# A second branch's output projection as two quads of seven products, with halves at both ends and a re-planned order

## The chip, the cores and the metric

The kernel runs on one core of a Trainium2 chip. The metric is the device time of one execution in microseconds (us); the time before is the median of three runs, 931.83 us (931.75 to 931.88).

## What is computed

One layer of a decoder trunk for 512 tokens of 1024 channels, in float32: three branches from one input projection, merged by gates, then a projection, then a feed-forward block, with RMS norms between.

```
h = rmsnorm(x);  proj = h @ w_in                    # 1024 -> 9216 columns
y_a = (gb * conv3(gc * v)) @ w_a_out                # branch 0
u   = conv31(u * sigmoid(ug)) + bias                # branch 1
y_b = silu(layernorm(u)) @ w_b_out
y_c = attention(q, rmsnorm(mem) @ w_kv) @ w_att_out # branch 2, 256 memory tokens
merged = sigmoid(p_g0)*y_a + sigmoid(p_g1)*y_b + sigmoid(p_g2)*y_c
x = x + merged @ w_o
x = x + (silu(gt) * up) @ w_down                    # gt, up: conv3 of rmsnorm(x) @ w_up, 2 x 2816
out = rmsnorm(x)
```

## The kernel before

**Numbers in two parts.** TensorE (PE) multiplies rounded operands (fp32r), so every operand is split: a high part, which is a rounding copy made by ScalarE (ACT), and a low part, the rest, made by a subtraction on VectorE (DVE). One product of two blocks is then three matmuls: high x high, high x low, low x high. For a weight unit of 128 x 1024 numbers this is `split_job` (L421): `high` (L444, ACT, tile `whi`) and `low` (L448, DVE, tile `wlo`). Where `lo_from` is given, ACT writes the negated high part instead, and a DMA issued by GpSimd's queue (POOL) adds the raw weights to it on the way, which leaves the low part.

**Seven products instead of eight.** The large projections run as quads: 1024 x 512 by 512 tokens is cut 2 x 2 x 2, and seven products of 24 matmuls of 256 columns (`multiply`, L612, matmul at L624) replace eight. The operands are sums of blocks: `form_jobs` (L527) makes them for the activations (t5, t7, t6, t4 are sums, b00, b10, b11 plain blocks), and `quad_loads` (L576) for the weights, either by DVE additions or, with `by_dma`, by accumulating DMAs from POOL's queue (`more`, L582). `quad_reads` (L643) puts the seven results from the PSUM banks together: copies on ACT (r1, r5, r6, r4), additions on DVE (r2, r7, r3).

**Order of the stages on PE.** Warm-up matmuls; keys and values of the memory (`keys_product`, `values_product`); eighteen mixer quads, with attention placed between their products; after the quads of the gates the output projections of the branches: `merge_product` (L1339) for branches 2 and 0, and, after the last product of the last gate quad, branch 1. A branch's projection is eight units, (m, g), of 24 matmuls of 512 columns each (L1349 to L1351). The conv over 31 taps runs on ACT and DVE beside the quads; its layer norm ends with two rows of statistics ("v") that PE brings to all partitions (L759), shortly before branch 1's projection: `lns` (L1261, DVE) scales, `swish` (L1268, ACT) applies the silu in place, `split_pair` (L1278 high, L1282 low) makes `ybh` and `ybl`. Behind each m come `weigh` (the gate times the bank, L1382) and `sum` into `mg` (L1400).

**From there on.** w_o as seven products a, b, f, c, d, e, g in this order (`pe_wo`, through `product`, L395 to L397; weights held in the freed operand tiles of the quads; `mgh` and `mgl` at L1500 and L1505; `ms` subtractions; rows x1 at L1560), the norm's transposes (L1586), eleven up quads whose start is written out by hand in `first`, conv3 and silu, then w_down as seven products with the rows read as they end (`read`, L1977), squared (L1982), a root (L1996), scaled on ACT and DVE (L2003, L2004) and written (L2008).

**What sets the order.** PE's order is a list written by hand (`seq`, and the table `beside`). All other work is a job with an engine, a cost, its inputs and its buffers; class `Jobs` (L99) places the jobs one after another on SP's queue, POOL's queue, ACT and DVE: `latest_starts` (L141) works back from PE's list when each is due, tables `LATER` and `AHEAD` shift kinds of jobs, `jobs.first` sets the first loads, and `transfer_end` models the two queues of transfers with the share `SHARE`. The instructions are issued in the order found, and each engine keeps it on the chip (`issue_in_program_order`, L81). So a wait of one instruction holds all that stand behind it on its engine.

## Time and profile before

| | |
|---|---|
| median of three runs | 931.83 us |
| the profiled execution | 931.52 us |
| its span, first to last instruction | 929.3 us |
| granted TensorE clock | 0.997 |
| PE busy | 916.8 us, 6644 matmuls |
| DVE busy | 837.3 us, 948 instructions |
| ACT busy | 672.5 us, 908 instructions |
| POOL busy | 126.5 us |
| DMA | 190.59 MB, mean 205 GB/s |

A row of the timeline has start, length, engine, line and operation, output and inputs, partitions x elements, a count where alike instructions are put together, and in brackets the idle time before it with what ended it. `bank` is a PSUM tile, `wf` a raw weight unit, `f..h` and `f..l` the parts of an operand. Lengths of matmuls overlap, since the next one starts before the last has drained; their starts tell the pace. The row of a stretch has its length, the busy time and count for each engine, the granted clock, the mean share of the 16 DMA engines and GB/s.

### The profile page before, as it was taken

The numbers are of one execution on the slowest core, as the hardware profiler recorded it, in microseconds if no ns is written. First come the engines' busy times: TensorE is split into PE (matmuls) and PEld (weight loads), VectorE is DVE, ScalarE is ACT, GpSimd is POOL, SyncE is SP. The second block draws the span as 40 slices with busy tenths as digits, with TensorE's granted clock in tenths as the row PEclk, the third lists the DMA queues.
The fourth block names the chain that finished last, engine by engine and source line by source line (L and its number), as shares of the span: only waits on it lengthen the run. The fifth ranks groups of instructions, "written<-read, shape, count | busy, mean of one in ns | idle before, by whom it ended". The sixth has DMA issues, their size and how long they took to land.

```text
span 929.3 us, 16689 instructions
## 1 busy us (share of the span) xinstructions
PE 916.8 (99%) x6644; PEld 860.5 (93%) x6644; DVE 837.3 (90%) x948; ACT 672.5 (72%) x908; POOL 126.5 (14%) x153
## 2 busy tenths in 40 slices
PE   8999999999999999999999999999999999999996
PEld 7999999999989999999899888898999999988885
DVE  6898999969889999999996778897899889999986
ACT  7676988759978879878856743766767676765655
POOL 0121111101111112110100011021211121002300
PEclk9999999999999999999999999999999999999998
DMA  9999678857676799967955598499999878779962
GB/s 356 371 269 236 137 171 178 201 133 136 170 185 170 177 191 243 210 174 183 226 115 158 186 314 179 97 246 295 258 226 235 209 141 166 195 268 329 251 125 91
DMA packets 54077, 190.59 MB, mean 205 GB/s; under 512 B 6128, under 2 KB 6256, under 8 KB 54000
## 3 DMA queue, kind: packets, MB, share of 16 engines
q0 software_dynamic: 20880, 75.24, 45.5%
q1 hardware_dynamic: 32400, 113.23, 34.0%
q8 instruction: 52, 0.85, 0.4%
q10 hardware_dynamic: 720, 1.06, 0.3%
q14 instruction: 25, 0.20, 0.1%
HBM read 185.31 MB, written 4.19 MB: 204 GB/s over the span
## 4 chain that ended last, share of the span: by engine, by line
PE 93%; DMA 3%; ACT 2%; DVE 1%; issue 1%; SPq 0%; ACTq 0%; POOLq 0%
PE bank L624 56%; PE bank L395 6%; PE bank L397 6%; PE bank L396 6%; PE bank L1349 5%; PE bank L1350 5%; PE bank L1351 5%; DMA wf<-in_w_up 2%; PE bank L871 2%; DMA mem<-in_mem_t 1%; ACT whi L444 0%; DVE wlo L448 0%; PE ss L750 0%; PE bank L1098 0%; ACT j L1982 0%
## 5 line engine op out<-in xcount | busy, mean ns | idle before, releaser
L444 ACT CAST whi<-wf 128x1024 fp32r<-128x1024 f32 (+1 forms) x195 | 202.9, 1044 | 100.9 <-PE bank L624 40.1
L448 DVE TENSOR_TENSOR wlo<-wf,whi 128x1024 fp32r<-128x1024 f32 (+1 forms) x189 | 228.3, 1214 | 29.8 <-ACT whi L444 29.4
L1170 ACT ACTIVATE tp<-u,pk 128x510 f32<-128x510 f32 (+22 forms) x184 | 119.7, 706 | 7.5 <-DVE acc L1177 6.5
L1177 DVE TENSOR_TENSOR acc<-acc,tp 128x1022 f32<-128x1022 f32 (+22 forms) x92 | 109.5, 1193 | 4.2 <-ACT tp L1170 2.4
L582 POOL DMA_DIRECT2D wf<-in_w_in x48 | 42.5, 894 | 229.7 <-DVE wlo L448 164.0
L624 PE MATMUL bank<-ft6h,wlo 128*128 128x256 f32 x232 | 64.4, 278 | 1.2 <-DVE wlo L448 1.2
L624 PE MATMUL bank<-ft6h,whi 128*128 128x256 f32 x232 | 64.6, 278 | 1.0 <-ACT gt L651 1.0
L624 PE MATMUL bank<-fb10h,whi 128*128 128x256 f32 x232 | 64.4, 278 | 0.0
L624 PE MATMUL bank<-fb00h,whi 128*128 128x256 f32 x232 | 64.4, 278 | 0.0
L624 PE MATMUL bank<-fb00l,whi 128*128 128x256 f32 x232 | 64.3, 277 | 0.0
L624 PE MATMUL bank<-fb00h,wlo 128*128 128x256 f32 x232 | 64.3, 277 | 0.0
L624 PE MATMUL bank<-ft7h,whi 128*128 128x256 f32 x232 | 64.3, 277 | 0.0
L624 PE MATMUL bank<-ft7l,whi 128*128 128x256 f32 x232 | 64.3, 277 | 0.0
L624 PE MATMUL bank<-ft7h,wlo 128*128 128x256 f32 x232 | 64.3, 277 | 0.0
L624 PE MATMUL bank<-fb11h,whi 128*128 128x256 f32 x232 | 64.3, 277 | 0.0
L624 PE MATMUL bank<-ft5h,wlo 128*128 128x256 f32 x232 | 64.2, 277 | 0.0
L624 PE MATMUL bank<-ft5h,whi 128*128 128x256 f32 x232 | 64.2, 277 | 0.0
L624 PE MATMUL bank<-ft5l,whi 128*128 128x256 f32 x232 | 64.2, 277 | 0.0
L624 PE MATMUL bank<-ft6l,whi 128*128 128x256 f32 x232 | 64.2, 277 | 0.0
L624 PE MATMUL bank<-fb10h,wlo 128*128 128x256 f32 x232 | 64.2, 277 | 0.0
L624 PE MATMUL bank<-fb10l,whi 128*128 128x256 f32 x232 | 64.2, 277 | 0.0
L624 PE MATMUL bank<-fb11l,whi 128*128 128x256 f32 x232 | 64.1, 276 | 0.0
(392 smaller groups left out, 3143.8 us busy)
## 6 DMA issues: line engine op xcount, KB each, us to landing
wf<-in_w_in SPq DMA_DIRECT2D x52, 512.0 KB, 4.9
wf<-in_w_in POOLq DMA_DIRECT2D x48, 512.0 KB, 5.8
wf<-in_w_up SPq DMA_DIRECT2D x29, 512.0 KB, 5.3
wf<-in_w_up POOLq DMA_DIRECT2D x28, 512.0 KB, 6.9
wf<-in_w_down SPq DMA_DIRECT2D x15, 512.0 KB, 4.2
wf<-in_w_v SPq DMA_DIRECT2D x8, 512.0 KB, 10.1
wf<-in_w_att_out SPq DMA_DIRECT2D x8, 512.0 KB, 3.9
wf<-in_w_a_out SPq DMA_DIRECT2D x8, 512.0 KB, 3.8
```

The costliest lines, as they stand in the source:

```text
L395: nc.tensor.matmul(ps, s_hi, w_hi, start=start, stop=False, skip_group_check=again)
L396: nc.tensor.matmul(ps, s_hi, w_lo, start=False, stop=False, skip_group_check=again)
L397: nc.tensor.matmul(ps, s_lo, w_hi, start=False, stop=stop, skip_group_check=again)
L444: nc.scalar.copy(parts[0], src())
L448: nc.vector.tensor_tensor(lo, src(), hi.bitcast(F32), op=ALU.subtract)
L582: nc.gpsimd.dma_start(out=tiles[key], in_=block(w, col[c], k), accum_op=ALU.add)
L624: nc.tensor.matmul(ps[:, c, :], w[:, k, at], a[k], start=first and n == 0, stop=i == 3 and n == 2, skip_group_check=again,)
L1170: nc.scalar.activation(two(("tp", p, s))[:, j, s:], two(("u", p))[:, j, : SEQ - s], AF.Copy, scale=weight(j),)
L1177: nc.vector.tensor_tensor(a, a, two(("tp", p, s))[:, :, s:], op=ALU.add)
L1349: nc.tensor.matmul(ps, w_hi[:, i, at], hi, start=first, stop=False)
L1350: nc.tensor.matmul(ps, w_hi[:, i, at], lo, start=False, stop=False)
L1351: nc.tensor.matmul(ps, w_lo[:, i, at], hi, start=False, stop=last)
```

## The change

1. Branch 1's projection leaves `merge_product`: its 1024 columns become two quads `("mq", 0)` and `("mq", 1)` through `quad_loads` (with `by_dma`), `multiply_job` on operand forms "y", and `quad_reads` without its last read. PE's order is f = 1, 5, 2, 6, 7, 4, 3, both quads in turn. The forms are made in halves of 512 columns (`y_parts`), the sums in place on `acc`.
2. `weigh` works on half the tokens of both channel blocks, from the tile `("y", m)`, once directly from the bank with a factor of -1.
3. Four low parts of w_o (products a and b) come by DMA (`WO_LOWS`).
4. The values' first unit (`V0`) is loaded, split and multiplied in halves, as the keys' first unit was before; `msq` waits for the high part of the values' second unit; `exp` waits for all four `sg`.
5. The last product "g" of w_down writes its second row tile into two banks of 256 columns, which are read, squared and summed by halves; row tile 1 is scaled after the read of row tile 0 of "g".
6. The planner: when a transfer is placed, the landing of the other queue's running transfer is set anew; ties are broken in a fixed order; some assumed costs differ (`SHARE`, `LOAD`, `MORE`, latencies), `LATER` and `AHEAD` have 91 entries instead of 24, `jobs.first` and the list `first` of the up quads are changed. The order on ACT, DVE and both queues is therefore different throughout.

```diff
-    for p in range(4):
-        split_pair(("acc", p), ("ybh", p), ("ybl", p), [("swish", p)])
+    def rows_of(p, r):
+        return two(("acc", p))[:, :, r * HALF : (r + 1) * HALF]
+    def y_parts(key, e, src, after, use):
...
+        def high():
+            if e == 0:
+                form_tile("y", key)
+            for at, h in pieces(form["y", key, "views"][0]):
+                nc.scalar.copy(h, src()[:, at, :])
+        def low():
+            hi, lo = form["y", key, "views"]
+            for (at, h), (_, l) in zip(pieces(hi), pieces(lo)):
+                nc.vector.tensor_tensor(l, src()[:, at, :], h.bitcast(F32), op=ALU.subtract)
...
+    for e in range(2):
+        top, end = ("acc", e), ("acc", 2 + e)
+        b00 = y_parts("b00", e, lambda e=e: rows_of(e, 0), done(e), [top])
+        b10 = y_parts("b10", e, lambda e=e: rows_of(2 + e, 0), done(2 + e), [end])
+        y_parts("b11", e, lambda e=e: rows_of(2 + e, 1), done(2 + e), [end])
...
+        job(Y5 + (e,), "DVE", dve(512), y5, ...)
+        job(("y", "t7", e), "DVE", dve(512), ...)
+        job(("y", "t6", e), "DVE", dve(512), ...)
+        job(("y", "t4", e), "DVE", dve(512), ...)
+        y_parts("t5", e, t5_half, [Y5 + (e,)], [Y5])
+        y_parts("t7", e, lambda e=e: rows_of(e, 1), [("y", "t7", e)], [top])
+        y_parts("t6", e, lambda e=e: rows_of(e, 0), [("y", "t6", e)], [top])
+        y_parts("t4", e, lambda e=e: rows_of(2 + e, 0), [("y", "t4", e)], [end])
...
+                quad = ("mq", m // 2)
+                if m % 2 == 0:
+                    quad_loads(quad, w_b_out, m * 256, m * 256 + 256, by_dma=True, lows=MQ_LOWS)
+                    quad_reads(quad, ("y", m), ("y", m + 1), ANY, all_but_4=True)
...
+                    def weigh_last(m=m, gate=gate, at=at, quad=quad):
+                        t = two(gate)[:, :, at]
+                        nc.vector.scalar_tensor_tensor(
+                            t, halves(("bank", quad, "a")), -1.0, t, op0=ALU.mult, op1=ALU.mult)
...
-        (GATE[1, 1], 3): lambda: [pe_merge(1, m) for m in range(4)],
+        (GATE[1, 1], 3): lambda: [
+            multiply_job(("mq", q), f, "y") for f in (1, 5, 2, 6, 7, 4, 3) for q in range(2)],
...
+    WO_LOWS = [(p, i) for p in "ab" for i in range(2)]
...
-            split_job(("wo", p, i), ("wo", key, i), 2, 512, [after], held=WO_HELD.get((p, i)))
+            split_job(("wo", p, i), ("wo", key, i), 2, 512, [after], held=WO_HELD.get((p, i)),
+                      lo_from=WO_SRC[p][i] if (p, i) in WO_LOWS else None)
...
+    halved_unit(K0, block(w_kv, 0, 0), 4)
+    halved_unit(V0, w_v[0, 0], 2)
...
+        if (hp, kp) == (0, 0):
+            for e in range(2):
+                pe(V0 if e else ("V0",), 6 * MM, lambda e=e: values_product(0, 0, e),
...
-        job(("msq", g), "ACT", actv(1024), mem_square, [("ldm", g, 0), ("ldm", g, 1)],
+        job(("msq", g), "ACT", actv(1024), mem_square,
+            [("ldm", g, 0), ("ldm", g, 1), ("wh", ("V", 0, 1))],
...
-                [("top", h, tp)] + ([("exp", h, 0)] if tp else []),
+                [("top", h, tp)] + ([("exp", h, 0)] if tp else [("sg", p) for p in range(4)]),
...
+    def end_steps(us, i):
+        for u in us:
+            hi, lo = w_units["pd", "g", u]
+            for k in range(PAIR_UNITS[u].start, PAIR_UNITS[u].stop):
+                ps = make(end_banks[i]) if k == 0 else tiles[end_banks[i]]
...
+            job(("sr", t, 0), "ACT", 0.4, lambda: square(last, 0, ENDS[0], ss_end),
+                [("rd", "end", 0)])
+            job("ends", "DVE", 0.1, first_end, [("sr", t, 0), ("hd", t)])
+            job(("sr", t, 1), "ACT", 0.4, lambda: square(last, 0, ENDS[1]), [("rd", "end", 1)])
...
+        job(("sc", t), "DVE", 0.95, lambda t=t: scaled(t),
+            [("rt", t)] + ([("rd", "g", 0)] if t == 1 else []))
...
-    def transfer_end(self, queue, start, cost):
+    def moved(self, queue, start):
...
+                slowed = "POOL" if e == "SP" else "SP"
+                if self.work[slowed] > 0.0 and self.moved(slowed, start) > free[slowed]:
+                    other = moving[slowed]
+                    free[slowed] = self.moved(slowed, start)
+                    ends[other] = free[slowed] + self.jobs[other][4]
```

More of the change, by code (lines that the diff above doesn't have):

```diff
@@ L218, in run @@
                 self.left[name][0] += 1
+        free = {e: 0.0 for e in ["PE"] + sorted({j[0] for j in self.jobs.values()} - {"PE"})}
         pe.reverse()
@@ L829, in hybrid_block_kernel, with halved_unit, high, low @@
-    first_parts = []
+    K0, V0 = ("K", 0, 0), ("V", 0, 0)
+    def halved_unit(unit, src, n_k):
+        s, raw, parts = unit[0], ("raw", unit), []
+        job(("raw tile", s), "NONE", 0.0, lambda: make(raw), take=[(raw, "wf")])
+        for e in range(2):
+            at = slice(512 * e, 512 * (e + 1))
+            job(("ld0", s, e), "SP", 0.7, lambda at=at: nc.sync.dma_start(
+                out=tiles[raw][:, at], in_=src[:, at]), [("raw tile", s)],
+                LOAD_LATENCY, use=[raw])
+            def high(e=e, at=at):
+                if e == 0:
+                    parts.extend(
+                        wts.tile([P, 1024], F32R, tag=s, name=name(s)) for s in ("whi", "wlo"))
+                    w_units[unit] = [t.rearrange("p (k n) -> p k n", k=n_k) for t in parts]
+                nc.scalar.copy(parts[0][:, at], tiles[raw][:, at])
+            def low(at=at):
+                hi, lo = parts
+                nc.vector.tensor_tensor(
+                    lo[:, at], tiles[raw][:, at], hi[:, at].bitcast(F32), op=ALU.subtract
+                )
+            job(("wh0", s, e), "ACT", actv(512), high,
+                [("ld0", s, e)] + ([("wh0", s, 0)] if e else []), use=[raw])
+            job(("wl0", s, e), "DVE", dve(512), low, [("wh0", s, e)], use=[raw])
@@ L1754, in hybrid_block_kernel @@
             pe_wo(p, i)
+    ENDS = [slice(0, 256), slice(256, 512)]
+    end_banks = [("bank", "end", i) for i in range(2)]
     def chain(p):
@@ L1764, in pe_down @@
         if u == 0 and before:
-            needs += [("rd", before, t) for t in range(2)]
+            needs += [("rd", before, t) for t in range(1 if p == "g" else 2)]
+        if p == "g":
+            banks = banks[:1] + (end_banks if u in (1, 2) else [])
         n, ts = (ps.stop - ps.start) * 6 * MM, range(2)
```

258 lines of the change are left out of this document (169 added, 89 removed), and 15 rows, old and new, of tables (AHEAD, LATER).

## The prediction

> **What bounds the kernel now.** I read the page's shares and its chain first, then the waits of PE, then stretches of time, and then single rows.
>
> ```profile
> span 929.3 us, 16689 instructions
> ...
> PE 916.8 (99%) x6644; PEld 860.5 (93%) x6644; DVE 837.3 (90%) x948; ACT 672.5 (72%) x908; POOL 126.5 (14%) x153
> ...
> PE 93%; DMA 3%; ACT 2%; DVE 1%; issue 1%; SPq 0%; ACTq 0%; POOLq 0%
> ```
> ```profile
> PE bank L624 <- DVE wlo L448: 1.2, 2, 0.8
> PE bank L624 <- ACT gt L651: 1.0, 2, 0.8
> PE bank L396 <- DVE wlo L448: 0.8, 1, 0.8
> ```
> ```profile
> 300.00:400.00 100.00, 100.00 (x883) 100.00 (x882) 99.10 (x107) 82.29 (x114) 17.37 (x20) 1.00 0.88 200
> 505.00:570.00 65.00, 65.00 (x314) 54.60 (x314) 51.86 (x56) 39.92 (x47) 4.98 (x6) 1.00 0.75 229
> 588.00:622.00 34.00, 34.00 (x246) 31.75 (x245) 29.33 (x35) 25.39 (x40) 5.89 (x7) 1.00 0.79 192
> 600.00:650.00 50.00, 47.76 (x402) 46.76 (x401) 42.46 (x49) 35.22 (x49) 9.49 (x11) 1.00 1.00 262
> ```
> The columns of the last fence are the stretch, its length, then busy time of PE, weight loads, DVE, ACT and POOL, the granted clock, the DMA share and GB/s. PE sets the time: it is busy for 99% of the span and waits for little. So two things count: matmul time that is removed, and every place where the operands for PE come later than it does. DVE is next, full to 99.10 of 100 us in the mixer quads (300 to 400), but with 13.1 us to spare from 505 to 570, which is where the change works. The run that was profiled took 931.52 us, 2.2 more than its span and 0.31 under the median; I sum against 931.52 and add 0.31 at the end.
>
> **1. The second branch's product in fourteen instead of sixteen parts.** Removed are 8 units of 24 matmuls of 512 columns (192); added are 14 products of 24 matmuls of 256 (336), the weight of 168.
>
> ```profile
> 502.60 0.28 PE L624 MATMUL bank<-ft7h,wlo 128*128 128x256 f32 x1
> ...
> 505.07 0.28 PE L624 MATMUL bank<-ft7h,wlo 128*128 128x256 f32 x1
> 505.19 0.60 PE L759 MATMUL rows<-ident,cols 128*128 128x128 f32 x4
> 505.54 0.48 PE L1349 MATMUL bank<-yah,whi 128*128 128x512 f32 x1
> ...
> 507.02 0.39 PE L1349 MATMUL bank<-yah,whi 128*128 128x512 f32 x1
> ...
> 510.88 0.39 PE L1351 MATMUL bank<-yah,wlo 128*128 128x512 f32 x1
> ```
> The modelled lengths overlap, so I go by starts. From 507.02 to 510.88 lie 17 steps of a 512-wide matmul: 0.227 each. In the 300 to 400 stretch 883 matmuls, nearly all 256 wide, take 100 us: 0.1133 each. So 192 x 0.227 = 43.6 becomes 336 x 0.1133 = 38.1: **-5.4 us**. The 256-wide rows are not always that quick: from 502.60 to 505.07 there are 21 steps of 0.1176, shortly after a 512-wide stretch. If all 336 went so, they'd take 39.5: bounds -5.5 to -4.0. I take the quick pitch, since the same quad is back to it 3 us after the short 512-wide stretch at 505.54.
>
> The Trainium skill, "TensorE: Matmul & The Clock Gate", section "Back-to-back issue gap", says that weight load and matmul together set the spacing, 81 ns at 128 columns and 131 ns at 512. Interpolated to 98 at 256, an estimate from that page, 336 would cost 32.9 against 25.2: the change would lose 7.8 us here instead. The trace disagrees (0.227 and 0.1133, one half of it).
>
> **2. What feeds it.** Before, each finished acc gets one high (ACT) and one low part (DVE) of 1024 columns, and eight weight units. After, fourteen products need fourteen weight units, fourteen half-wide high and low parts, eight half-wide sums, and reads that combine banks: 81 DVE instructions stand between the first `lns` and the low part of w_o's third product "f" (28 of 1024 columns, 51 of 512, 2 of 256), all in front of it on DVE.
>
> ```profile
> 506.00 4.61 DVE L1261 TENSOR_TENSOR acc<-acc,rows 128x1024 f32<-128x1024 f32 x4
> 510.52 1.22 DVE L448 TENSOR_TENSOR wlo<-wf,whi 128x1024 fp32r<-128x1024 f32 x1
> 511.65 2.36 DVE L1282 TENSOR_TENSOR ybl<-acc,ybh 128x1024 fp32r<-128x1024 f32 x2
> ...
> 596.19 0.68 DVE L1604 TENSOR_TENSOR fb00l<-bank,fb00h 128x512 fp32r<-128x512 f32 x1
> 596.79 0.68 DVE L1604 TENSOR_TENSOR fb10l<-bank,fb10h 128x512 fp32r<-128x512 f32 x1
> ```
> ```profile
> 506.34 1.28 ACT L1268 ACT_TABLE_LOAD   x1
> 507.63 2.94 ACT L1268 ACTIVATE acc<-acc,pk 128x512 f32<-128x512 f32 x4
> ...
> 519.58 1.28 ACT L1373 ACT_TABLE_LOAD   x1
> 520.88 1.34 ACT L1373 ACTIVATE g<-g,pk 128x512 f32<-128x512 f32 x2
> ```
> ```profile
> L448 DVE TENSOR_TENSOR wlo<-wf,whi 128x1024 fp32r<-128x1024 f32 x7 | 8.6, 1222 | 4.5 <-ACT whi L444 4.5
> ```
> From 506.00 to 511.65 lie five instructions of 1024 columns, 1.13 each (1.135 over longer runs of them); 596.19 to 596.79 gives 0.60 per 512; 256 columns are estimated at 0.34 from the two. The sum is 28 x 1.135 + 51 x 0.60 + 2 x 0.34 = 63.1 us, so from 506.00 DVE is done at 569.1 at the earliest. In the same clock PE has, from 505.54 to product "f", 24 x 0.227 (last half of the first branch), 2 x 24 x 0.1133 (the gate quad's last products), 336 x 0.1133, and 48 x 0.227 (w_o's "a" and "b") = 59.9: it arrives at 565.4. **PE must wait there for at least 3.7 us.** Before, eight 512-wide units in place of the fourteen products made this cover 65.3 us, and DVE had 13.1 of the 65 from 505 to 570 to spare. A wait of PE for a or b, if any, is part of this one and not added to it.
>
> On top come waits of DVE inside the stretch. ACT changes there four times between the tables of silu and sigmoid (before: two), and half of `ft7h` and half of `b10`, `b11` stand behind such a change. A load is 1.28. Lower bound: all hidden, 0; upper bound: the two further changes in full, 2.6. Waits for ACT are not rare: in the seven rows of the last fence (515 to 570) DVE waited 4.5 us for high parts, though it had time then. I take one load's worth, between the ends, since ACT has spare time before some of them: **+5.0** (3.7 to 6.3).
>
> The Trainium skill, "ScalarE: Activation LUTs", section "What ACT_TABLE_LOAD costs", adds a drain of some 1380 ns to each switch, 2.66 in all. By that, two further switches would put up to 2.8 more on ACT here, an estimate from that page; the trace agrees with the load (1.28) but the work after it starts 0.01 to 0.02 us later.
>
> **3. Loads.** Eight accumulating DMAs build weight sums that DVE would else add; four lows of w_o are moved from DVE to ACT and POOL's queue.
>
> ```profile
> q0 software_dynamic: 20880, 75.24, 45.5%
> q1 hardware_dynamic: 32400, 113.23, 34.0%
> ```
> ```profile
> 620.67 1.05 ACT L444 CAST whi<-wf 128x1024 fp32r<-128x1024 f32 x1 [1.85 <-DMA wf<-in_w_up]
> ...
> 631.74 1.05 ACT L444 CAST whi<-wf 128x1024 fp32r<-128x1024 f32 x1 [2.63 <-DMA wf<-in_w_up]
> 635.41 1.99 ACT L444 CAST whi<-wf 128x1024 fp32r<-128x1024 f32 x2 [2.62 <-DMA wf<-in_w_up]
> ```
> Queue q0, POOL's accumulating DMAs, takes 0.455 x 929.3 us for 75.24 MB: 2.95 us for one of 0.524 MB, so the twelve cost 35 us of DMA time. From 505 to 570 a quarter of the DMA's time is free (share 0.75), and loads go ahead of PE by their buffers; so I cost them nothing there. Without this cover they come back one for one. At the up quads' start (600 to 650) the DMA is full (1.00) and PE loses 2.24 us, mostly behind high parts that waited 1.85, 2.63 and 2.62 us for `in_w_up`. Standing 5 us at "f" gives the transfers that time: I take -1.7 (0 to -2.24). Against it, DVE comes out of "f" with no lead. From 588 to 622 it was idle for 34.00 - 29.33 = 4.7 us in waits that cost PE nothing; now some of them do: +1.1, a quarter (0 to 4.7). Together **-0.6** (-2.2 to +4.7).
>
> **4. The start.** V's first unit now comes in halves, and the square of mem goes behind it.
>
> ```profile
> 9.91 0.41 PE L395 MATMUL bank<-whi,mh 128*128 128x512 f32 x1
> 11.09 0.50 PE L396 MATMUL bank<-wlo,mh 128*128 128x512 f32 x1 [0.77 <-DVE wlo L448]
> ```
> ```profile
> 7.78 1.05 ACT L734 ACTIVATE msq<-mem 128x1024 f32<-128x1024 f32 x1
> 8.74 3.16 ACT L444 CAST whi<-wf 128x1024 fp32r<-128x1024 f32 x3
> ```
> 9.91 to 11.09 should be 0.227, so 0.95 is lost on the low part; its high part (8.74) stood behind `msq` (7.78). With a half copy first and `msq` gone, the half low is there before 9.91. **-0.95** (0 to -1.2, the rest being smaller waits of the keys).
>
> **5. The end.** The last product's second row tile is cut into two halves with own banks; 33 matmuls of 512 become 66 of 256, no change in PE time (33 x 0.227 against 66 x 0.1133).
>
> ```profile
> 921.53 0.39 PE L397 MATMUL bank<-whi,zl 128*128 128x512 f32 x1
> ...
> 922.02 0.75 DVE L2004 SCALAR_TENSOR_TENSOR x<-x,cols,gfin 128x512 f32<-128x512 f32 x1
> 922.69 0.68 DVE L1977 TENSOR_TENSOR x<-x,bank 128x512 f32<-128x512 f32 x1
> ...
> 923.41 0.63 ACT L1982 ACTIVATE j<-x 128x512 f32<-128x512 f32 x1 [0.66 <-DVE x L1977]
> ```
> The last read (922.69) waits for the scaling of another row tile (922.02), then a square and a root follow. Halves shorten read and square by some 0.3 each, but row tile 1's scaling now stands on DVE between the last read and the last scaling (0.75). **-0.2** (0 to -1.0).
>
> The rest (retuned order on ACT, DVE and the queues, `exp` behind all `sg`) I cost at nothing: in the mixer quads DVE is full and each of its instructions is still there. If the new order loses lead in one place there, it costs up to what such a place shows elsewhere, 0 to +3.
>
> **Sum.** 931.52 - 5.4 + 5.0 - 0.6 - 0.95 - 0.2 = 929.4, and with 0.31 for the median **929.7 us**.
>
> **Rivals.**
> - *DVE's reserve is gone (slower).* Both further table loads reach DVE (6.3 at "f"), the 4.7 us of waits after it, which now have no cover, all reach PE, and the loads' waits stay. 931.83 - 5.4 - 0.95 - 0.2 + 6.3 + 4.7 = 936.3. It decides as soon as the lateness from `lns` to the up quads exceeds the 6.55 us gained, and shows as slower from 8.4. For it: 63.1 against 59.9 before any wait. Against: ACT is the lighter engine there (39.92 of 65 us).
> - *Only the bare shortage (faster).* DVE never waits: 3.7 at "f", the loads' 2.2 gone, nothing after: 931.83 - 5.4 - 0.95 - 0.2 + 3.7 - 2.2 = 926.8; with the end's full 1.0 saved, 926. For it: in 505 to 570 ACT is busy for only 39.92 us, so it can be ahead of DVE. Against: the 4.5 us that DVE waited for high parts with time to spare.
> - *DMA is the bound.* The 35 us don't fit: up to 570 some 16 us are free, and the remainder meets the share of 1.00 from 600 on. If a quarter of that, 5 us, gets past the buffers to PE besides the 5.0: 935. For it: 1.00 at the up quads. Against: "f" itself gives it 5 us.
> - *Narrow products stay at 0.1176* as from 502.60 to 505.07: 39.5 for 38.1, 931.1. Against: the 883 of the mixer quads. (The Trainium skill, "TensorE: Matmul & The Clock Gate", points this way.)
> - *The halves at start and end don't do what they are for*: no 0.95, no 0.2: 930.9. Against: 8.74 is directly behind 7.78's square on ACT.
>
> **How the numbers follow.** Forecast 0.43, reserve gone 0.21, bare shortage 0.20, DMA 0.08, narrow 0.03, halves 0.05. A measurement of this kernel tells about 0.2% from no change, 1.9 us: faster is under 930.0, slower over 933.7. The forecast's own spread (928 to 932) lies about two thirds under 930.0: 0.28 with the 0.20 of the bare shortage makes 0.48 faster; 0.15 + 0.08 makes 0.23 within; 0.29 slower. The range 925.5 to 936.0 reaches from the bare shortage to just short of the slower case's centre; half of that case and a tail below, some 0.15, are left out.
>
> **What would show it.** In the changed profile: `y` products at 0.1133; a wait of PE of 4 to 6 us for a DVE `mgl` or `wlo` at w_o's third product, with DVE full from `lns` on; less than 1.5 us lost in the first 50 us of the up quads; no wait at V's first unit; the last read within 0.3 us of the last matmul's end. I am wrong if PE doesn't stop at "f" (then the order of DVE isn't the bound that I take it for, and 925 or less follows), or if the wait goes on into the up quads.

## The result and the profile after

| | before | after |
|---|---|---|
| median of 7 runs each | 931.79 us (930.85 to 931.94) | 935.10 us (932.81 to 935.78) |
| the profiled execution / its span | 931.52 / 929.3 us | 935.50 / 933.7 us |
| granted clock of the profiled execution | 0.997 | 0.995 |

The ratio is 1.0032, with an interval of 1.0023 to 1.0042: the change makes the kernel 0.3% slower. The forecast was 929.7.

The page of the changed kernel: the span, the busy times and the shares of the chain that ended last.

```profile
span 933.7 us, 17138 instructions
...
PE 916.0 (98%) x6821; PEld 866.9 (93%) x6821; DVE 851.4 (91%) x979; ACT 689.5 (74%) x941; POOL 137.1 (15%) x165
...
PE 86%; DVE 5%; ACT 5%; DMA 2%; issue 1%; SPq 0%; ACTq 0%; DVEq 0%
```

PE is busy for 916.0 us, only 0.8 less than before, although 5.4 us of matmul time were removed: matmuls at half clock (below) are busy for longer. The span has grown by 4.4 us, and in the chain of the work that ended last PE's share fell from 93 to 86%, while DVE's and ACT's rose from 1 and 2 to 5 each. The second view is what PE waited for: engine and line, the work it waited for, then us in total, times, longest.

```profile
PE bank L431 <- DVE mgl L1649: 3.3, 1, 3.3
...
PE bank L659 <- ACT g L709: 1.2, 1, 1.2
PE bank L659 <- DVE y L435: 1.0, 1, 1.0
...
PE bank L659 <- DVE fb10l L1369: 0.6, 1, 0.6
```

There are two groups. The first row stands where the forecast put its one wait, at w_o's third product "f". The rows of L659 stand inside the two new quads, where the forecast had no wait. Third, the stretches:

```profile
515.00:570.00 55.00, 51.73 (x393) 48.17 (x391) 52.35 (x71) 44.60 (x59) 9.55 (x11) 1.00 0.97 252
568.00:573.30 5.30, 1.98 (x10) 1.10 (x8) 5.30 (x7) 3.17 (x4) 2.64 (x3) 0.88 0.99 345
573.30:578.60 5.30, 5.30 (x13) 4.14 (x14) 5.30 (x6) 2.09 (x2) 0.00 (x0) 0.50 1.05 299
600.00:650.00 50.00, 50.00 (x410) 49.03 (x409) 42.85 (x49) 34.76 (x50) 8.66 (x10) 1.00 0.93 229
```

From 515 to 570 PE is busy for 51.73 of 55 us. From 568 to 573.3 it works for 1.98 of 5.3. From 573.3 to 578.6 it is "busy" for the whole 5.3 us and issues only 13 matmuls, at a granted clock of 0.50. The single rows show what that is:

```profile
569.58 0.40 PE L430 MATMUL bank<-wlo,mgh 128*128 128x512 f32 x1
573.29 0.79 PE L431 MATMUL bank<-whi,mgl 128*128 128x512 f32 x1 [3.32 <-DVE mgl L1649]
573.89 0.63 PE L429 MATMUL bank<-whi,mgh 128*128 128x512 f32 x1
...
578.58 0.52 PE L431 MATMUL bank<-whi,mgl 128*128 128x512 f32 x1
```

The step from 569.58 to 573.29 should be 0.227: 3.5 us are lost. From 573.89 to 578.58 lie 11 steps of 0.427 instead of 0.227 each; with the one step before and the one after, 2.7 us more. One wait is paid for twice. The Trainium skill, "TensorE: Matmul & The Clock Gate", section "What's actually happening", says that the clock falls to half after an idle window of about 3.4 us and comes back after a busy one of that length; section "HAM oscillation — how this bites in real kernels" shows transfers doing it to a kernel again and again. The trace agrees with the half (0.50): the matmuls are slow for 5 us, and the granted clock is 0.50 from 572.01 to 578.84, which is twice 3.41 us.

The two profiled spans differ by 4.4 us. Taken from the starts of matmuls in both traces against the paces 0.227 and 0.1133, and from the rows above, it comes about so:

| term | us |
|---|---|
| 336 narrow matmuls for 192 wide ones | -5.4 |
| the start (first 25 us) | -1.1 |
| waits inside the two quads | +4.3 |
| wait at "f" | +3.5 |
| half clock behind it | +2.7 |
| wait for `x1` ahead of the up quads | +1.0 |
| the up quads, from their first matmul to their last (600 to 650: 2.24 lost before, nothing after; small waits behind 650) | -2.0 |
| w_down, first matmul to last; of it 0.4 are the halves of its last product, which go at 0.12 | +0.8 |
| from the end of the last matmul to the end of the span (7.4 before, 8.0 after) | +0.6 |

**Why PE waits in the quads.** These are ACT's rows from the sigmoids on; between the first and the last there is no pause, each row starts as the one before it ends.

```profile
503.60 2.56 ACT L1489 ACTIVATE g<-g,pk 128x512 f32<-128x512 f32 x4
...
507.13 1.28 ACT L1322 ACT_TABLE_LOAD   x1
...
518.75 1.28 ACT L1489 ACT_TABLE_LOAD   x1
...
523.87 1.28 ACT L1322 ACT_TABLE_LOAD   x1
...
533.03 1.28 ACT L1489 ACT_TABLE_LOAD   x1
...
535.57 0.61 ACT L1364 CAST ft7h<-acc 128x512 fp32r<-128x512 f32 x1
```

So from 503.6 to 535 ACT, not DVE, is the engine that is full. DVE stands behind it, as its own rows say; the last time it is the low part `ft7l`, which waits for its high part:

```profile
536.21 0.69 DVE L1369 TENSOR_TENSOR ft7l<-acc,ft7h 128x512 fp32r<-128x512 f32 x1 [1.05 <-ACT ft7h L1364]
```

DVE's waits for ACT from the first `lns` on are 1.6, 1.5 and 1.1, together 4.2 us. The chain that ended last says the same: from 501.24 on it lies on ACT, from 536.21 on DVE, and neither PE nor a transfer is in it again before 573.29.

**Why PE waits at "f".** From 536.21 on DVE has no pause. The last product of the quads ends on PE about 558.06; then PE has only w_o's "a" and "b", 48 x 0.227 = 10.9 us. DVE has, from the read that runs as this product ends (`y<-y,bank`) to the first `mgl`, 16.5 us:

```profile
549.78 1.22 DVE L482 TENSOR_TENSOR whol<-wo,whoh 128x1024 fp32r<-128x1024 f32 x1
...
556.73 0.68 DVE L693 TENSOR_TENSOR y<-y,bank 128x512 f32<-128x512 f32 x1
...
570.89 1.22 DVE L482 TENSOR_TENSOR whol<-wo,whoh 128x1024 fp32r<-128x1024 f32 x1
572.02 2.35 DVE L1649 TENSOR_TENSOR mgl<-mg,mgh 128x1024 fp32r<-128x1024 f32 x2
```

The first of the two `mgl` takes 1.22 us and ends at 573.24; PE goes on at 573.29. DVE started 1.3 us ahead of PE's 558.06, and PE has two matmuls of "f" (0.5) and two breaks between products (0.3) before it needs `mgl`: 16.5 - 1.3 - 10.9 - 0.8 = 3.5, which is what is lost there. As neither engine pauses in between, this had to add up: it tells where the time went, and not which part of DVE's work would have to be less. The two rows `whol` are w_o's "d", which a run below leaves out.

### The profile page after: what moved, and what is told of

It is laid out like the page before. It is cut to its first block, busy times and chain, and to the rows that moved or that the text cites. A ratio compares the mean times of both kernels' runs of the same rounds, so it can differ in the third digit from the quotient of the medians.

```text
span 933.7 us, 17138 instructions
## 1 busy us (share of the span) xinstructions
PE 916.0 (98%) x6821; PEld 866.9 (93%) x6821; DVE 851.4 (91%) x979; ACT 689.5 (74%) x941; POOL 137.1 (15%) x165
## 4 chain that ended last, share of the span: by engine, by line
PE 86%; DVE 5%; ACT 5%; DMA 2%; issue 1%; SPq 0%; ACTq 0%; DVEq 0%
PE bank L659 56%; PE bank L431 6%; PE bank L429 6%; PE bank L430 6%; PE bank L1465 3%; PE bank L1464 3%; PE bank L1466 3%; PE bank L915 2%; DVE wlo L482 2%; ACT whi L478 1%; DMA wf<-in_w_up 1%; ACT acc L1322 1%; DMA wf<-in_w_v 1%; DVE mg L1539 0%; PE ss L788 0%
## 5 line engine op out<-in xcount | busy, mean ns | idle before, releaser
L478 ACT CAST whi<-wf 128x1024 fp32r<-128x1024 f32 x202 | 210.7, 1045 | 92.0 <-PE bank L659 39.9
L482 DVE TENSOR_TENSOR wlo<-wf,whi 128x1024 fp32r<-128x1024 f32 (+1 forms) x196 | 235.9, 1210 | 23.4 <-ACT whi L478 23.1
L1231 DVE TENSOR_TENSOR acc<-acc,tp 128x988 f32<-128x988 f32 (+22 forms) x92 | 109.1, 1187 | 8.8 <-ACT tp L1224 7.4
L659 PE MATMUL bank<-fb10h,whi 128*128 128x256 f32 x248 | 69.0, 278 | 1.7 <-ACT g L709 1.2
L659 PE MATMUL bank<-fb10l,whi 128*128 128x256 f32 x248 | 68.7, 277 | 0.6 <-DVE fb10l L1369 0.6
L659 PE MATMUL bank<-ft6h,whi 128*128 128x256 f32 x248 | 68.8, 278 | 0.2 <-ACT gt L686 0.2
L659 PE MATMUL bank<-fb11h,wlo 128*128 128x256 f32 x248 | 68.6, 277 | 0.3 <-DVE wlo L482 0.3
L659 PE MATMUL bank<-fb00h,whi 128*128 128x256 f32 x248 | 68.8, 277 | 0.0
L659 PE MATMUL bank<-ft7h,whi 128*128 128x256 f32 x248 | 68.7, 277 | 0.0
L659 PE MATMUL bank<-ft7l,whi 128*128 128x256 f32 x248 | 68.7, 277 | 0.0
L659 PE MATMUL bank<-ft7h,wlo 128*128 128x256 f32 x248 | 68.7, 277 | 0.0
L659 PE MATMUL bank<-fb00l,whi 128*128 128x256 f32 x248 | 68.7, 277 | 0.0
L659 PE MATMUL bank<-ft6l,whi 128*128 128x256 f32 x248 | 68.7, 277 | 0.0
L659 PE MATMUL bank<-fb00h,wlo 128*128 128x256 f32 x248 | 68.7, 277 | 0.0
L659 PE MATMUL bank<-ft6h,wlo 128*128 128x256 f32 x248 | 68.7, 277 | 0.0
L659 PE MATMUL bank<-ft5h,wlo 128*128 128x256 f32 x248 | 68.7, 277 | 0.0
L659 PE MATMUL bank<-ft5h,whi 128*128 128x256 f32 x248 | 68.7, 277 | 0.0
L659 PE MATMUL bank<-ft5l,whi 128*128 128x256 f32 x248 | 68.7, 277 | 0.0
L659 PE MATMUL bank<-fb11h,whi 128*128 128x256 f32 x248 | 68.7, 277 | 0.0
L659 PE MATMUL bank<-fb10h,wlo 128*128 128x256 f32 x248 | 68.6, 277 | 0.0
```

The source lines that it names most:

```text
L478: nc.scalar.copy(parts[0], src())
L482: nc.vector.tensor_tensor(lo, src(), hi.bitcast(F32), op=ALU.subtract)
L659: nc.tensor.matmul(ps[:, c, :], w[:, k, at], a[k], start=first and n == 0, stop=i == 3 and n == 2, skip_group_check=again,)
L1231: nc.vector.tensor_tensor(a, a, two(("tp", p, s))[:, :, s:], op=ALU.add)
```

## The experiments

The theory after the result: (A) ACT's full stretch makes the quads' waits; (B) the wait at "f" is set only by what DVE has to do behind the last product of the quads; (C) standing there halves the clock. The rivals: the forecast's own step, that one sum of DVE's work from `lns` on sets the lateness; that the accumulating DMAs are the cause; that the wait alone, without the clock, makes the time. Times are compared by the ratio to the kernel before in the same runs (931.35 to 931.75); 0.001 is 0.93 us, and each interval reaches about 0.001 to either side. Lines behind an edit are shifted by up to three.

### The clock: fillers at "f"

Six matmuls of 512 columns whose result is overwritten, issued ahead of "f", where PE would stand:

```diff
+                for _ in range(6 if (p, k, t) == ("f", 0, 0) else 0):
+                    nc.tensor.matmul(ps, four(("mgh", p))[at], w_hi[:, 0, :], start=True, stop=True)
```

> The changed kernel with six more matmuls of 512 columns (their result is overwritten, the output is unchanged) at the head of w_o's third product, where PE stood 3.3 us and then ran twelve matmuls at 0.43 instead of 0.23 under a granted clock of 0.50. Theory clock (the half pace is the price of standing idle for too long): the six fit into the wait, 2 us of it remain, the pace behind it stays 0.23, and the time falls by 2.4 to about 932.7, with less spread between executions. Rival (the pace is set by transfers or by something else at that place): the pace stays 0.43 and the time stays at 935.1 or gains nothing beyond noise.

Measured 934.26 (932.78 to 935.05), ratio 1.0031 [1.0019, 1.0043]. Six are too few: they last 1.4 us, 2.0 us of the wait remain, and the median stays. In the profiled execution (932.78) no matmul at "f" ran at half clock, and its mean granted clock is 0.998. Four of the six executions have 0.996, so in most of them the half clock seems to be still there. So the same with fourteen, 3.2 us:

> As the run with six added matmuls at the head of w_o's third product, but with fourteen of them (3.2 us, overwritten, output unchanged), so that next to nothing of the wait of 3.3 to 3.5 us is left. With six of them 2.1 us were left, and the median fell by only 0.8, since a wait of that length halves the clock in some executions, as those with reordered work show. Theory clock: no half pace at w_o in any execution, 2.4 less than 935.1, about 932.7, unless the waits in the quads (3 us within 5) do it too. Rival (the pace isn't from standing idle): 935 or more, as the added matmuls cost what they take.

Measured 932.82 (932.16 to 934.03), ratio 1.0016 [1.0007, 1.0025], 1.5 us less than the changed kernel by the ratios, 2.3 by the medians. The stretches from 570 to 600, first of the changed kernel, then of this one:

```profile
570.00:600.00 30.00, 25.91 (x105) 20.90 (x106) 25.49 (x30) 16.42 (x22) 5.24 (x6) 0.89 0.97 257
```
```profile
570.00:600.00 30.00, 29.05 (x133) 23.39 (x132) 27.88 (x32) 17.24 (x24) 5.24 (x6) 1.00 0.94 256
```

The clock is 1.00 instead of 0.89, and nothing but matmuls without use was added. (C) holds, with about 2 us. Part of the spread goes with it: of the changed kernel's seven executions the one with a mean granted clock of 0.998 took 932.81, the six with 0.995 and 0.996 took 933.55 to 935.78. It isn't all of the spread, since the eleven of this run, at 0.997 and 0.998, still lie between 932.16 and 934.03.

### The order on DVE and at the end

Three shifts in the planner's tables or inputs. First, `lns` is due earlier, so that ACT gets `acc` sooner:

```diff
-    "DVE h t4": 6, "DVE h t5": 463, "DVE kt": 120, "DVE lns": 109, "DVE ms c": -4, "DVE r2 q": 20,
+    "DVE h t4": 6, "DVE h t5": 463, "DVE kt": 120, "DVE ms c": -4, "DVE r2 q": 20,
```

> The changed kernel without the planner's entry that puts two of the four lns late: all four stand at the head of the stretch on DVE, so that silu's four pairs can follow each other on ACT. Theory ACT (the lateness of the quads begins with ACT: sigmoids, table loads and silu ahead of the first operands, DVE waits 1.6 and 1.5 us for it): these two waits go, the waits of PE inside the quads (4.2 us) fall to under 2, the one at w_o's third product falls to 1 us, no half clock: 3 to 5 less, 930 to 932. Rival DVE (the sum of DVE's work from lns to the third product alone sets it): it starts and ends as before, the waits only move, 935.

Measured 933.63 (932.09 to 934.33), ratio 1.0021 [1.0012, 1.003]. The wait at "f" fell to 2.1 and the one for `g` rose to 2.0, and 1.7 for `wlo` and 1.3 for the transposes came up. And still, behind a wait of 2.1 us, the clock was halved in the profiled execution:

```profile
571.00:576.00 5.00, 5.00 (x16) 3.93 (x15) 5.00 (x6) 1.44 (x2) 0.04 (x1) 0.66 1.05 292
```

Second, `mgl` and `ms` of "f" go ahead of other work on DVE:

```diff
 LATER = {
+    "DVE mgl f": -30, "DVE ms f": -30,
```

> The changed kernel with the low part of w_o's third operand and its difference 30 us more urgent for the planner: the same work on DVE, but about four instructions (1.1 us each) that nothing needs so soon stand behind that low part. Theory order (what counts is only the work between the last quad product and the third product, 16.5 us on DVE against 10.9 us of cover): the wait falls from 3.3 to about 1.3 us, the clock isn't halved, 4 us less, 931. Rival sum (all the work from lns on sets it): the wait stays at 3.3, 935. If only the wait falls and the half clock stays: 933.

Measured 933.33 (931.85 to 934.88), ratio 1.0017 [1.0009, 1.0026].

```profile
PE bank L1731 <- DVE xnorm L1723: 2.0, 1, 2.0
...
PE bank L432 <- DVE mgl L1650: 1.1, 1, 1.1
```
```profile
600.00:604.00 4.00, 4.00 (x15) 3.53 (x16) 3.17 (x5) 2.15 (x4) 0.86 (x1) 0.59 0.96 182
```

The wait at "f" falls by 2.2, and 2.0 come up at the norm's transposes, with the half clock behind them (0.59 in those 4 us). DVE's lateness is moved, not removed: "f" is only the first place that shows it.

Third, "ends", a small sum on DVE, comes behind the last read instead of ahead of it:

```diff
-            job("ends", "DVE", 0.1, first_end, [("sr", t, 0), ("hd", t)])
+            job("ends", "DVE", 0.1, first_end, [("sr", t, 0), ("hd", t), ("rd", "end", 1)])
```

> The changed kernel with the tiny sum of two squares (ends) behind the last read instead of ahead of it. Theory end (the last read of 256 columns stood on DVE behind ends, which waited 0.96 us for ACT): the last read starts at the end of the last matmul, 0.5 to 0.9 less, 934.4. Rival (row tile 1's scaling on ACT sets the end): the same 935.1.

Measured 933.83 (932.34 to 935.68), ratio 1.0025 [1.0015, 1.0035]: 0.6 less, within the interval of nothing; the trace tells more. This is the end of the changed kernel:

```profile
924.74 0.28 PE L431 MATMUL bank<-whi,zl 128*128 128x256 f32 x1
...
925.46 0.28 PE L431 MATMUL bank<-whi,zl 128*128 128x256 f32 x1
...
926.43 0.42 DVE L2160 TENSOR_TENSOR x<-x,bank 128x256 f32<-128x256 f32 x1
...
926.95 0.72 ACT L2191 ACTIVATE x<-x,cols 128x512 f32<-128x512 f32 x1 [0.63 <-DVE cols L2190]
...
928.12 0.42 ACT L2163 ACTIVATE j<-x 128x256 f32<-128x256 f32 x1 [0.44 <-ACT x L2191]
```

The last read starts 0.97 after the last matmul, behind a small DVE job ("ends") that waits for ACT; then ACT scales row tile 1 (926.95) before the last square (928.12), which its operand allowed from 926.85. In this run the last read starts 0.71 after the last matmul and the final scaling 2.95 instead of 3.7 after it. The scaling still stands ahead of the square, so only a part is won. The first two rows show one thing more: from 924.74 to 925.46 lie six steps of 0.12, where the narrow matmuls of the new quads go at 0.1133. The last product's 66 halves take 7.9 us in place of 33 x 0.227 = 7.5. Why they are slower is open.

### The rival "one sum from `lns` on"

Low parts of weights are left out: the high part is used in their place, so the numbers that come out are others. With the order unchanged, DVE has 4 x 1.13 = 4.5 us less to do: once in the quads' products 1 and 2, once in 4 and 3, which are the last, and once, 2 x 1.13, in w_o's "d", whose low parts DVE makes late: one at 549.78, some 8 us ahead of the end of the last product, and one at 570.89, directly ahead of `mgl`.

```diff
             hi, lo = parts
+            if unit[0][0] == "mq" and unit[1] in (1, 2):
+                w_units[unit] = [w_units[unit][0]] * 2
+                return
```

> The changed kernel in its own order, but the low parts of the weights of quad products 1 and 2 are left out (their third matmul takes the high part instead): four instructions of 1.135 us less on DVE, early in the stretch. Theory sum (the prediction's: DVE is the bound from lns to w_o's third product): 4.5 less on DVE, the wait of 3.3 goes and with it the half clock: 929 to 930. Theory ACT first (until about the quads' seventh product DVE waits for ACT): DVE only waits longer for ACT, PE's waits stay 2.9, 1.1 and 3.3: 935, within 1.

Measured 934.82 (934.07 to 935.85), ratio 1.0035 [1.0022, 1.0048]: no gain. PE's waits are those of the changed kernel, and DVE's additions on `acc` (L1394 there, L1397 here) only stand longer behind ACT, 2.9 us instead of 1.5. All of DVE's waits for ACT in the stretch grow from 4.2 to 8.4, by nearly all that was left out. A group's row has line, operation, count, busy time and mean, then the idle time before it and what ended it.

```profile
L1394 DVE TENSOR_TENSOR acc<-acc,acc 128x512 f32<-128x512 f32 x2 | 1.4, 689 | 1.5 <-ACT acc L1322 1.5
```
```profile
PE bank L431 <- DVE mgl L1652: 3.3, 1, 3.3
```
```profile
L1397 DVE TENSOR_TENSOR acc<-acc,acc 128x512 f32<-128x512 f32 x2 | 1.4, 694 | 2.9 <-ACT acc L1325 2.9
```

Now products 4 and 3 (the same edit with `in (4, 3)`):

> The changed kernel in its own order, but the low parts of the weights of quad products 4 and 3 are left out (their third matmul takes the high part instead): 4 x 1.135 us less on DVE, between DVE's last wait for ACT (at the seventh product) and the last quad product. Theory: the wait of 1.1 at product 4 goes; what DVE gains beyond that it loses waiting for the banks of the last product, so that the third product's wait stays at about 3 us since its time runs from there: 933.5 to 935. Rival (DVE's sum up to the third product sets it): the wait goes, 4.5 us and the half clock less: 929.

Measured 933.61 (931.52 to 937.06), ratio 1.0024 [1.0014, 1.0034]. The wait for `y` at product 4 is gone; at "f" PE still stands 3.3. Of the 4.5 us that DVE won it lost 2.8 standing, 1.35 for high parts from ACT and 1.45 for a bank, with PE as the one it waits for. `mgl` starts 1.6 us earlier (570.39, before 572.02), but as PE isn't held at product 4, it comes to "f" 1.6 earlier too:

```profile
545.87 0.69 DVE L435 SCALAR_TENSOR_TENSOR y<-bank,y 128x512 f32<-128x512 f32 x1 [1.45 <-PE bank L662]
```

And w_o's "d" (`unit[:2] == ("wo", "d")`):

> The changed kernel in its own order, but the two low parts of the weights of w_o's product d are left out (its third matmul takes the high part instead): 2 x 1.135 us less on DVE, both behind the point from which DVE no longer waits for ACT, one of them directly in front of the low part that PE waits for. Where the same four instructions left out early changed nothing, theory DVE-late (from the quads' seventh product on DVE alone sets the third product's start) expects here the full effect: the wait falls by 2.3 from 3.3 to about 1.0, no half clock: 4 to 5 less, 930.5. Rival (the low part waits for the bank reads behind the last quad product, not for DVE's work): wait and time stay, 935.

Measured 931.91 (930.54 to 934.38), ratio 1.001 [1.0001, 1.0019].

```profile
PE bank L431 <- DVE mgl L1652: 1.2, 1, 1.2
```

2.3 us taken from DVE late take 2.1 from the wait; 4.5 us taken earlier took none, twice. That refutes the forecast's sum, by which the wait falls in all three runs. It doesn't bear out (B) either: half of the 2.3 lay ahead of the end of the last product and counted nearly in full. The trace gives another line between the runs. DVE's time is won for "f" where DVE then stands for nothing else, as here, where its waits are those of the changed kernel; in the other two it stood 4.2 and 2.8 longer. The time falls by 2.0 by the ratios, less than the theory's 4 to 5: the clock's part comes back in some executions (0.996 and 933.46 to 934.38 in three of eleven, 0.997 or 0.998 and at most 932.11 in the others).

### ACT's tables

The sigmoid of branch 1's last gates is replaced by a silu, so that ACT changes tables three times less (the gates' values are others then):

```diff
-                        t, t, AF.Sigmoid, bias=par("b_gate", br * KC + 2 * m + j)
+                        t, t, AF.Silu if br == 1 and m > 1 else AF.Sigmoid,
+                        bias=par("b_gate", br * KC + 2 * m + j)
```

> The changed kernel in its own order, but the sigmoid of the second branch's last two gates is replaced by silu, so that ACT changes its table once instead of four times in the stretch: 3 x 1.28 = 3.8 us less on ACT (the gate's values are not the reference's). Theory ACT first: the waits at the quads fall from 4.2 to under 1.5 us, the one at w_o's third product to about 2, half clock seldom: 930 to 932. Theory sum on DVE: PE's waits together stay at 7.7: 935.

Measured 932.96 (930.57 to 934.84), ratio 1.0012 [1.0004, 1.0021].

```profile
PE bank L431 <- DVE mgl L1650: 3.3, 1, 3.3
...
PE bank L429 <- ACT mgh L1645: 1.2, 2, 1.0
...
PE bank L659 <- ACT g L709: 0.7, 1, 0.7
```

3.8 us less on ACT take the quads' waits from 4.3 to 1.4 by the starts (of the listed ones 0.7 for `g` is left), which is (A). "f" keeps its 3.3, since `mgl` and PE's arrival both come 1.3 us earlier, and a part of the gain is lost at w_o's "a", for `mgh`.

### The DMA: four accumulating transfers fewer, four more

First, w_o's four lows go back to DVE; in another run the quads' products 1 and 2 get theirs by DMA too.

```diff
-    WO_LOWS = [(p, i) for p in "ab" for i in range(2)]
+    WO_LOWS = []
```

> The changed kernel with the four low parts of w_o's first two products made on DVE again instead of by accumulating transfers. Theory DVE (after the last quad product DVE has more to do than PE gives it time for): four times 1.135 more in front of w_o's third product, longer waits there, 938 to 942. Rival DMA (the twelve further accumulating transfers are what delays): faster, under 934.

Measured 947.04 (946.22 to 948.0), ratio 1.0166 [1.0152, 1.0179]. The waits are now 5.7 for `mgh`, 2.5 for the up quads' `gt`, 2.4 for `mgl`, and behind the 5.7 the granted clock is 0.50 for 10.24 us. That is more than the theory gave; the order on both engines is a new one, and how much of it is that order's is open. That w_o's four transfers cost the time isn't borne out: without them, with their low parts on DVE, it is worse. The eight transfers of the quads' sums were not taken out in any run; against them as the cause stands the chain above, which has no transfer between 501 and 573.

```diff
-    MQ_LOWS = ()
+    MQ_LOWS = (1, 2)
```

> The changed kernel with the low parts of the weights of quad products 1 and 2 made by four more accumulating transfers (2.95 us of DMA time each) in place of DVE. The DMA's share is 0.97 between 515 and 570. Theory: twelve further accumulating transfers just fit and sixteen don't; the quads' weights come late and PE waits for low parts: 938 to 945. Rival (DMA has room, DVE is the bound in the quads): 4.5 us less on DVE, under 933.

Measured 947.6 (946.55 to 949.48), ratio 1.0173 [1.016, 1.0187].

```profile
PE bank L659 <- DMA wlo<-in_w_b_out: 3.6, 2, 2.6
```
```profile
515.00:570.00 55.00, 45.53 (x346) 44.34 (x345) 40.73 (x56) 42.61 (x58) 13.05 (x15) 0.91 1.03 251
```

With four more the DMA share is 1.03 from 515 to 570, and PE stands for transfers themselves, besides 7.1 for `wlo` and 2.4 for `whi`; the granted clock of the stretch is 0.91. In the changed kernel the share was 0.97 there: the twelve of the change fit, just.

### The start alone

The kernel before with nothing but the halves of V's first unit and the moved square:

> The kernel before with one part of the change alone: the values' first unit in halves with its own loads, and the square of mem behind the second unit's high part. The wait of 0.95 us at the values' first unit goes, the rest stays: 930.8, 1.0 less than before. Rival (the start is bound by what it loads, and the gain is given back in the first 30 us): 931.7.

Measured 931.01 (930.26 to 931.78), ratio 0.9996 [0.9988, 1.0005].

```profile
600.00:650.00 50.00, 47.15 (x385) 46.58 (x384) 41.13 (x47) 34.13 (x47) 9.52 (x11) 0.97 1.00 267
```

In the first 25 us 1.9 us less are lost. But PE gives it back where DMA is full (share 1.00 from 600 to 650): busy for 47.15 us against 47.76, and at a granted clock of 0.97. In this execution the clock is 0.50 from 638.04 to 641.46, and PE issues 17 matmuls there against 32 in the kernel before: 1.7 us more. It has the lowest mean clock of the eleven (0.996), so the others may have given back less; the whole 1.9 would be a ratio of 0.998, which lies outside the interval. So a gain at the start can be lost again in a later stage, by standing there and by the clock.

### The corrections together

`lns` and `mgl f` as above (`ms f` by -6 only), the end as above, `ACT sigmoid` at 30 instead of 32.54; and in a second kernel seven fillers each ahead of w_o's "a" and "f":

> The same corrected orders without the added matmuls. Against the run with them it shows the clock alone: if waits of about 2 us at w_o's first and third product already halve the clock in part of the executions, it is up to 2.4 slower than that run and spreads more; if only waits beyond 3 us do, both are equal.

> The changed kernel with four orders of work corrected in the planner's tables (all lns at the head; w_o's third low part and its difference earlier; sigmoid a little earlier, so that the last two gates' come as one; the end's tiny sum behind the last read) and seven 512-wide matmuls (overwritten, output unchanged) each at the head of w_o's first and third product, so that PE never stands for 2 us. If lateness by order and the half clock together took away the gain: 4 to 6 less than 935.1, so 929 to 931, faster than before too. If the quads cost DVE more than PE saves whatever the order: no better than 932.

Without the fillers 931.85 (931.1 to 932.99), ratio 1.0 [0.9991, 1.0009]; with them **929.66** (928.73 to 930.6), ratio 0.9978 [0.9969, 0.9987]. First the waits and a stretch without fillers, then a stretch with them, whose longest wait there is 1.2 for `mgh`:

```profile
PE bank L430 <- ACT mgh L1645: 2.5, 1, 2.5
PE bank L432 <- DVE mgl L1650: 1.5, 1, 1.5
```
```profile
568.00:576.00 8.00, 6.46 (x17) 4.83 (x18) 8.00 (x9) 4.19 (x4) 1.30 (x2) 0.57 1.05 269
```
```profile
568.00:576.00 8.00, 7.42 (x32) 5.87 (x33) 8.00 (x9) 4.34 (x5) 1.21 (x2) 1.00 1.04 265
```

The two kernels differ in nothing but fourteen useless matmuls, and these save 2.2 us: the clock in that stretch goes from 0.57 to 1.00. With orders of its own and the clock held, the change is worth 0.2% against the kernel before; the remainder of the quads' 5.4 still goes into waits (1.2, 0.8, 0.4) and into standing that is filled (3.2). Whether another plan gets that too was not tried.

## Why the prediction was wrong, by its own steps

The range (925.5 to 936.0) held the time; the forecast did not, nor its sign.

- **What bounds the kernel.** Right in general: PE sets the time, and later operands cost. "DVE is next" was the wrong engine for the first 30 us of the stretch.
- **1. Fourteen narrow products: right.** -5.4. The rival at 0.1176 fell for the quads:

```profile
555.79 0.28 PE L659 MATMUL bank<-fb11l,whi 128*128 128x256 f32 x1
...
557.95 0.28 PE L659 MATMUL bank<-fb11h,wlo 128*128 128x256 f32 x1
```

  19 steps in 2.16 us are 0.1137 each.
- **2. What feeds it: the step that failed.** It forecast one wait of 5.0 at "f" out of one sum: DVE's work, 63.1 from 506.00 on, against PE's 59.9 from 505.54 on, which makes 3.7, and 1.3 (0 to 2.6) for DVE's own waits for ACT. It had no wait of PE inside the quads; of one at "a" or "b" it said that it "is part of this one and not added to it". The 81 instructions of DVE are right, and PE did stop at "f", for 3.5. The mis-sized term is DVE's waits for ACT: 4.2, not 1.3. I had called ACT the lighter engine with 39.92 of 65 us, a share of a stretch of which ACT fills the first part without a pause. With 4.2 the sum gives 7.9, and PE's waits at the two places together are 7.8. So the sum is right as an account, and wrong as a cause: 4.5 us fewer on DVE changed nothing at "f" (both runs that leave out low parts of the quads), because DVE then stood longer for ACT and for banks; 2.3 fewer, at 549.78 and 570.89, changed it by 2.1. The agreement of 3.5 with the bare 3.7 is chance. In place of the step there are three terms: 4.3 in the quads, from ACT; 3.5 at "f", from DVE's late work; and 2.7 from the clock. 10.5 instead of 5.0.
- **The clock had no term at all.** I forecast that PE would stand for 5 us and priced it at 5 us, although the clock's column stood in the rows that I read. However a wait of 5.0 falls into windows of 3.41 us, at least 2.5 of it lie in one of them, and in the traces every window with that much standing is followed by half clock (last section). The Trainium skill, "TensorE: Matmul & The Clock Gate", section "What's actually happening", has the rule that was missing, an idle window of about 3.4 us. By it one window at half the clock would have put the forecast 1.7 us later, an estimate from that page.
- **3. Loads.** Cover for the twelve transfers: right, and no more than that (0.97; 1.03 with four more). The up quads' start: -1.7 forecast, -2.0. DVE without lead: +1.1 forecast, +1.0 at `x1` (a quarter of 4.7 is 1.2, and step 2's cover before adds up to 65.4; nothing hangs on either):

```profile
599.35 0.50 PE L429 MATMUL bank<-whi,mgh 128*128 128x512 f32 x1 [0.80 <-DVE x L1704]
```

- **4. The start: right.** -0.95 forecast, -1.1. V's first low part is there when PE comes; 9.06 to 9.28 is the plain pace:

```profile
9.06 0.39 PE L429 MATMUL bank<-whi,mh 128*128 128x512 f32 x1
9.28 0.39 PE L430 MATMUL bank<-wlo,mh 128*128 128x512 f32 x1
```

- **5. The end: wrong.** -0.2 forecast, +0.6 behind the last matmul and +0.4 in the last product. I counted row tile 1's scaling on DVE; what costs is "ends" ahead of the last read, and the same tile's scaling on ACT ahead of the last square. And I counted the 66 halves at 0.1133, as no change in PE's time; they go at 0.12.
- **The rivals.** "DVE's reserve is gone" gave 936.3, near the 935.1, and half of its mechanism was there: the table loads did reach DVE and PE, since three loads fewer took 2.9 from the quads' waits. But it had 6.3 at "f" and 4.7 behind it, against 3.5 and 1.0, and neither the quads nor the clock, so its nearness is luck. For "DMA is the bound" the trace has nothing: no transfer lies in the chain from 501 to 573. "Only the bare shortage" fell with step 2.

## What to carry to other kernels

Matmul time that is removed counts only if the engines that make the operands keep up, and that is to be checked for every engine and piece by piece, with what each piece waits for. One sum over the whole stretch hides which engine is late where, and what an engine saves counts only if it doesn't stand for another one instead. A forecast that lets PE stand for 2 us or more has to price the half clock that may follow, and fillers that keep PE busy were a cheap cure here. A gain at the start can be given back in a later stage.

## What was not expected of the hardware

The half clock doesn't begin with the wait or at its end. In the run with only the end's edit, PE goes on at 573.12 after 3.3 us, runs four matmuls at the plain pace, and only from 574.15 on does it slow down; the granted clock is 0.50 from 574.24 to 577.65. In every kept trace the half clock ahead of the last matmul lasts 3.41 us, or twice or three times that, and the changes of one trace lie whole multiples of 3.41 us apart. That is a clock that looks at windows of its own. The Trainium skill, "TensorE: Matmul & The Clock Gate", section "What's actually happening", says the same (free-running, 3.4 us).

But a window need not be idle throughout. Here are the window ahead of the changed kernel's half clock, and then the two windows into which the wait of 2.0 us with six fillers falls:

```profile
568.60:572.01 3.41, 1.37 (x6) 0.63 (x4) 3.41 (x4) 2.54 (x3) 1.88 (x3) 1.00 1.03 375
```
```profile
568.53:571.94 3.41, 2.49 (x11) 1.56 (x9) 3.41 (x4) 2.34 (x3) 2.12 (x3) 1.00 0.94 370
571.94:575.36 3.42, 2.37 (x10) 1.98 (x11) 3.42 (x4) 0.00 (x0) 0.53 (x1) 1.00 0.93 322
```

In the first PE works for 1.37 us and stands for 2.0; half clock follows. With six fillers the wait lies across an edge, 0.9 us in one window and 1.0 in the next, and the clock stays. With `mgl` moved a wait of the same 2.0 us, at the transposes, lies in one window (596.43 to 599.84), and half clock follows. Counted over all sixteen kept traces up to the last matmul: after all thirteen windows at full clock in which PE stood for 1.98 us or more comes half clock, and after none with 1.3 or less. Of three in between, those with 1.59 and 1.82 were followed by it, one with 1.73 was not. Back to full speed it went after windows in which PE stood for 0.03 us at most; after those with 1.0 or more it stayed at half.

So waits shorter than 3.4 us do it too, when most of such a wait falls into one window. That this is also why executions of one kernel differ would fit, but isn't shown: one execution of each was traced.
